# S5 products of a batch pair in rows that alternate between the two halves of TensorE, with the states one chunk late

## The chip, the cores and the metric

The kernel runs on one core of a Trainium2 chip (TensorE, VectorE, ScalarE, GpSimd and SyncE beside 16 DMA engines). The metric is the device time of one execution in microseconds.

## What is computed

A two-layer decoder trunk over 256 tokens of width 1024. Layer 0 is a SwiGLU feed-forward, a mixer made of two parallel parts (a Mamba-2 SSD and an S5), a second feed-forward and a gated input embedding; layer 1 is the same with another mixer. Only S5 is touched. In the reference it is

```python
lam_bar = jnp.exp(lam * dt)
b_bar = ((lam_bar - 1.0) / lam)[..., None] * lax.complex(b_re, b_im)
bu = jnp.einsum('blgp,gnp->blgn', ug, b_bar)
_, states = lax.associative_scan(linear_recurrence_combine, (a, bu), axis=1)
y = jnp.real(jnp.einsum('blgn,gpn->blgp', states, c)) + d_skip * ug
```

with 64 groups of 16 channels and 64 complex states per group.

## The kernel before

The 256 tokens are cut into 64 chunks of 4 steps. The 64 groups are handled as 8 batches of 8 groups; a batch is 4 (`NP`) pairs of groups, one group on partitions 0 to 63, the other on 64 to 127 (`row_half`, L496). Every S5 product on TensorE is therefore a 64x64 by 64x64 product in fp32 that uses one half of the rows and the same half of the columns of the array; in the trace one product is two weight loads and two matmuls.

There are three kinds of these products.

- **W products (L543, tile `s5w`)**: in `s5_params`, for each batch, two matrices (i = real, imaginary) are turned over by a product with the identity into the PSUM tiles `tp[0]` and `tp[1]` (tag `tr`, two buffers, which the feed-forward's transposes `ht` use too). They run during the first feed-forward, one batch per step f of it, beside that step's VectorE work on the S5 tables. There the two tiles are the two halves of the alternation.
- **v products (L684, tile `s5v`)**: in `s5_batches`, called by `recur(0)` to `recur(3)` in the mixer with two batches (e = 0, 1), 32 products per call for each of the two: chunk inputs times W, into `v[0]` and `v[1]` (tag `mm`, two buffers).
- **y products (L712 with T and U, L715 with Q and S)**: at the end of `s5_batches`, 24 products per batch and call into `y[0]` and `y[1]` (tag `mm` again). T times U is the part inside a chunk and starts each accumulation; two products (real, imaginary) of Q with the states S follow. A chunk needs the states at the end of the chunk before it, so L715 writes columns 1 to 63 of y and reads columns 0 to 62 of S.

Between v and y VectorE works, first for e = 0 and then for e = 1 (they share the single buffers `rotm` and `rw`): four operations turn v by a table (L694 to L697, `rotc`, `rots`, `rotm`), two scans carry the states along (L702, `rw`), four operations turn them back into S (`rovc`, `rovs`, `S`). ScalarE copies y into G (L719). G goes through a Gelu (L725) and DRAM, and becomes the input of the `glu` products (L758 to L760).

The engines' instruction orders are not written out by hand. A planner with a modelled clock sends out, for each engine, the instruction that is ready first in its model, earlier program text ahead of later; instructions that write the same tile keep their order. So between S5 products stand products of the projections (`pc_bc`, `pc_xs`, `pj_z`) where the planner finds them ready. `behind` (L90) adds an order without a semaphore between two instructions of one engine. On the chip each engine's queue is then fixed.

Weights come by the SP queue in 1 MB units (`wst`), are cast by ScalarE to `wh` (L61) and completed by VectorE to `wl` (L62); each unit is two of each. Beside them VectorE does the convolutions (L811) in the mixer.

Of the kernel before, what the change touches and what calls it, by code (L numbers as in the profile page):

```python
# [8 lines left out]
F32 = mybir.dt.float32  # L9
# [8 lines left out]
P = 128  # L18
# [71 lines left out]
def behind(g, ins, anchors):  # L90

    for a in anchors:
        if a.engine == ins.ins.engine:
            g.tc.add_manual_dep(ins.ins, a.name, mybir.DependencyInfo(mybir.DependencyClass.NoSync,
                                                                      mybir.DependencyReason.DATA), reason="issue_after")
# [239 lines left out]
NP = 4  # L335
# [164 lines left out]
def s5_params(g, b, half):  # L500


    nc = g.nc
    mul, add, sub = ALU.mult, ALU.add, ALU.subtract
    c3, e3, bp, z = half
    ps = slice(NP * b, NP * b + NP)
    hs = slice(NP * (b % 4), NP * (b % 4) + NP)
    tmp = [g.s5p.tile([P, 2, NP * 80], F32, tag=f"s5t{i}", name=f"s5t{i}_{b}", bufs=1) for i in range(2)]

    def cmul(out, a, br, bi, shape):  # L510

        t0, t1 = (t[:, :, 0:out.shape[2]] for t in tmp)
        for t, at, v in ((t0, 0, br), (t1, 1, bi)):
            for i in range(2):
                nc.vector.tensor_tensor(t[:, i].rearrange(shape[0], **shape[1]), a(at, i), v, op=mul)
        nc.vector.tensor_tensor(out, t0, t1, op=add)

    LE, LQ = g.s5L
    powers = lambda L, i: L[:, i, :, ps].rearrange("p t q -> p q t")
    E = g.s5p.tile([P, 2, 256], F32, tag="s5e", name=f"s5e_{b}", bufs=2)  # L520
    cmul(E, lambda at, i: bc(e3[:, (1 - at) + i, hs], 3, 4), bc(powers(LE, 0), 2, 16), bc(powers(LE, 1), 2, 16),
         ("p (q c t) -> p q c t", dict(q=NP, t=4)))
    pk = g.s5p.tile([P, PACK - PACK_PE], F32, tag="s5pk", name=f"s5pk_{b}", bufs=2)
    Q = pk[:, 768:].rearrange("p (a n) -> p a n", a=2)
    cmul(Q, lambda at, i: bc(c3[:, at + i, hs], 2, 5), bc(powers(LQ, 0), 3, 16), bc(powers(LQ, 1), 3, 16),
         ("p (q t c) -> p q t c", dict(q=NP, t=5)))
    fine, coarse = (lambda i: bc(z[:, i, hs, 0:8], 2, 8)), (lambda i: bc(z[:, i, hs, 8:16], 3, 8))
    cmul(pk[:, 0:512].rearrange("p (a n) -> p a n", a=2), lambda at, i: fine((1 - at) + i), coarse(1), coarse(2),
         ("p (q a b) -> p q a b", dict(q=NP, a=8)))
    dec = pk[:, 512:768].rearrange("p (q c) -> p q c", q=NP)  # L530
    nc.scalar.copy(dec, bc(g.s5f[2][:, ps], 2, 64))
    nc.gpsimd.memset(dec[:, :, 0:1], 0.0)
    nc.gpsimd.dma_start(g.s5dram[b][:, PACK_PE:], pk)

    def rest():
        W, K = g.s5pe
        Ev, Qv = (x.rearrange("p a (q n) -> p a q n", q=NP) for x in (E, Q))
        tp = [g.ps.tile([P, NP, 64], F32, tag="tr", name=f"s5w_{b}_{i}", bufs=2) for i in range(2)]
        for turn in range(2):
            for q in range(NP):  # L540
                for i in range(2):
                    r = row_half(turn ^ i)
                    nc.tensor.matmul(tp[i][r, q, :], Ev[r, i, q, :], g.ident[r, r], start=True, stop=True)  # L543
        for i in range(2):
            nc.scalar.copy(W[:, i], tp[i])
        kp = g.ps.tile([P, 64], F32, tag="tr", name=f"s5k_{b}", bufs=2)
        for q in range(NP):
            for i in range(2):
                nc.tensor.matmul(kp[32 * q:32 * q + 32, :], bp[:, i, hs.start + q].rearrange("p j c -> p (j c)"),
                                 Qv[:, i, q, 0:64], start=i == 0, stop=i == 1)  # L550
        nc.vector.scalar_tensor_tensor(K[:, 48:64], g.cst("fold"), g.cols("s5d")[:, b:b + 1], kp[:, 0:16], op0=mul,
                                       op1=add)
        nc.scalar.copy(K[:, 64:112], kp[:, 16:64])
        nc.gpsimd.dma_start(g.s5dram[b][:, 0:PACK_PE], W.rearrange("p a q c -> p (a q c)"))
        for st in range(4):
            nc.gpsimd.dma_start(g.s5T[b][:, st, :], K[:, 16 * (3 - st):16 * (3 - st) + 64])

    return rest
# [75 lines left out]
    return ap.rearrange("p k (s c) -> p k s c", s=4)  # L634


def s5_inputs(g, pool, U, c):

    nc = g.nc
    uT = g.lnp.tile([P, 4, NTOK], F32, tag="ln_r", name=f"uT_{c}")  # L640

    def keep(h, ps):
        k = slice(2 * h, 2 * h + 2)
        if h:
            nc.vector.tensor_copy(by_step(uT[:, k, :]), ps.rearrange("p k (c s) -> p k s c", s=4))
        else:
            nc.scalar.copy(by_step(uT[:, k, :]), ps.rearrange("p k (c s) -> p k s c", s=4))

    if c:
        project_channels(g, f"u{c}", keep)  # L650
    else:
        channel_tiles(g, pool, f"u{c}", keep)
    d = g.perm[0][c]
    nc.gpsimd.dma_start(d.rearrange("(p k) n -> p k n", k=4), uT)
    dv = d.rearrange("(q r k) (s n) -> r k q s n", q=4, k=4, s=4)
    for st in range(4):
        to = U[st:P:4, 16 * c:16 * c + 16, :].rearrange("p (k q) n -> p k q n", q=4)
        nc.gpsimd.dma_start(to, dv[:, :, :, st, :])


def s5_batches(g, pool, U, G, bs):

    nc = g.nc
    mul, add, sub = ALU.mult, ALU.add, ALU.subtract
    W, T, Q, tab, S = [], [], [], [], []
    for b in bs:
        dram = g.s5dram[b]
        W.append(pool.tile([P, 2, NP, 64], F32, tag="W", name=f"W_{b}", bufs=3))  # L670
# [5 lines left out]
        Q.append(pool.tile([P, 2, NP, 80], F32, tag="Q", name=f"Q_{b}", bufs=3))  # L676
        nc.scalar.dma_start(Q[-1], dram[:, 1280:1920].rearrange("p (a q c) -> p a q c", a=2, q=NP))
    v = [g.ps.tile([P, 2, NP, 64], F32, tag="mm", name=f"s5v_{b}", bufs=2) for b in bs]
    for turn in range(2):
        for i in range(2):  # L680
            for q in range(NP):
                for e, b in enumerate(bs):
                    r = row_half(turn ^ e)
                    nc.tensor.matmul(v[e][r, i, q, :], W[e][r, i, q, :], U[r, NP * b + q, :], start=True, stop=True)  # L684

    for e, b in enumerate(bs):
        cosT, sinT, dec = (tab[e][:, 256 * i:256 * i + 256] for i in range(3))
        w = pool.tile([P, 2, 256], F32, tag="rw", name=f"rw_{b}", bufs=1)

        def rotate(src, name, out, ops):  # L690

            c = pool.tile([P, 2, 256], F32, tag="rotc", name=f"{name}c_{b}", bufs=2)
            s = pool.tile([P, 2, 256], F32, tag="rots", name=f"{name}s_{b}", bufs=2)
            nc.vector.tensor_tensor(c, src, bc(cosT, 1, 2), op=mul)  # L694
            nc.vector.tensor_tensor(s, src, bc(sinT, 1, 2), op=mul)
            for i in range(2):
                nc.vector.tensor_tensor(out[:, i], c[:, i], s[:, 1 - i], op=ops[i])  # L697

        m = pool.tile([P, 2, 256], F32, tag="rotm", name=f"rotm_{b}", bufs=1)
        rotate(v[e].rearrange("p a q c -> p a (q c)"), "rot", m, (add, sub))  # L700
        for i in range(2):
            nc.vector.tensor_tensor_scan(w[:, i], dec, m[:, i], 0.0, op0=mul, op1=add)  # L702
        S.append(pool.tile([P, 2, NP, 64], F32, tag="S", name=f"S_{b}", bufs=2))
        rotate(w, "rov", S[-1].rearrange("p a q c -> p a (q c)"), (sub, add))
    y = [g.ps.tile([P, NP, 64], F32, tag="mm", name=f"s5y_{b}", bufs=2) for b in bs]
    for turn in range(2):
        for q in range(NP):
            for i in range(-1, 2):
                for e, b in enumerate(bs):
                    r = row_half(turn ^ e)  # L710
                    if i < 0:
                        nc.tensor.matmul(y[e][r, q, :], T[e][r, q, :], U[r, NP * b + q, :], start=True,  # L712
                                         stop=False)
                    else:
                        nc.tensor.matmul(y[e][r, q, 1:64], Q[e][r, i, q, 16:80], S[e][r, i, q, 0:63],  # L715
                                         start=False, stop=i == 1)
    for e, b in enumerate(bs):
        lo = NP * b % 16
        nc.scalar.copy(G[:, lo:lo + NP, :], y[e])  # L719
# [252 lines left out]
def ab_inputs(g, pool, s5pool, yh, yl):  # L972

    nc = g.nc
# [34 lines left out]
    U = s5pool.tile([P, 32, 64], F32, tag="U", name="U", bufs=1)  # L1009
    for c in range(2):  # L1010
        s5_inputs(g, pool, U, c)
    yT = []

    def recur(n):
        if n % 2 == 0:
            half.append(pool.tile([P, 16, 64], F32, tag="G", name=f"G_{n // 2}", bufs=1))
        s5_batches(g, s5pool, U, half[-1], (2 * n, 2 * n + 1))
        if n == 1:
            yT.append(s5_half_out(g, half[-1], 0, yh, yl))

    half = []
# [513 lines left out]
```

## Time and profile before

| | us |
|---|---|
| median of 3 runs (1238.2 to 1241.11) | 1238.76 |
| the profiled execution | 1242.7 |
| its span, first to last instruction | 1240.9 |
| W products run from | 71.3 to 202 |
| v and y products run from | 256.5 to 367 |
| busy PE / DVE / ACT / POOL | 1210.4 / 854.5 / 583.9 / 72.4 |

PE is TensorE's matmuls, DVE VectorE, ACT ScalarE, POOL GpSimd. A matmul's own duration in the trace overlaps with its neighbours', so the pace is read from the starts, or from the chain of work that ended last, which counts each stretch of time once.

### The profile page before, as it was taken

What the parts mean: (1) busy time and instruction counts of PE and PEld (TensorE: products, weight loads), DVE (VectorE), ACT (ScalarE), POOL (GpSimd) and SP (SyncE); (2) the same over time, 40 slices, a digit from 0 to 9 for tenths busy, and PEclk for the clock granted to TensorE, in tenths of its full rate; (3) what the DMA queues carried; (4) which work ended last, traced back from release to release, by engine and by line L of the source; (5) the groups of instructions that cost most, each with busy time, mean ns of one, the idle gap of its engine ahead of it and who ended that gap; (6) DMA issues with size and microseconds to landing.
All of it is one profiled execution on the core that took longest, in us unless ns stands there. A gap on an engine that the chain in (4) does not pass through costs nothing.

```text
span 1240.9 us, 17250 instructions
## 1 busy us (share of the span) xinstructions
PE 1210.4 (98%) x6786; PEld 1005.9 (81%) x6786; DVE 854.5 (69%) x1352; ACT 583.9 (47%) x866; POOL 72.4 (6%) x124
## 2 busy tenths in 40 slices
PE   7999999999998999999998999999999999999998
PEld 6877777899887878888887888888888877888886
DVE  6999894688878766555567555456779776545466
ACT  5644452545535535443435444443674625444434
POOL 0012122110203000000000000000100010000000
PEclk9999999899999999999999999999999999999999
DMA  7567676775722647555536555554633327555532
GB/s 282 203 233 251 230 243 229 267 250 175 219 95 66 220 146 252 179 198 179 195 136 203 204 190 184 198 177 168 224 135 107 133 77 247 194 186 187 192 147 102
DMA packets 44609, 232.74 MB, mean 188 GB/s; under 512 B 9680, under 2 KB 10352, under 8 KB 20848
## 3 DMA queue, kind: packets, MB, share of 16 engines
q1 hardware_dynamic: 30672, 206.06, 48.2%
q0 software_dynamic: 4688, 14.16, 3.6%
q10 hardware_dynamic: 9168, 11.42, 2.8%
q8 instruction: 53, 0.87, 0.3%
q14 instruction: 28, 0.23, 0.1%
HBM read 219.56 MB, written 12.06 MB: 187 GB/s over the span
## 4 chain that ended last, share of the span: by engine, by line
PE 90%; DVE 4%; DMA 3%; ACT 2%; issue 1%; ACTq 0%; SPq 0%; DVEq 0%
PE gu_f L178 38%; PE acc_f L72 7%; PE acc_f L71 6%; PE acc_f L70 6%; DMA wst<-in_wall_dram 2%; PE pj_z L178 2%; PE ht_f L215 2%; DVE wl L62 2%; PE s5y L715 1%; PE acc_ab L72 1%; PE acc_ab L71 1%; PE acc_ab L70 1%; PE pj_u L178 1%; PE s5w L543 1%; PE pj_hg L178 1%; PE pj_gr L178 1%
## 5 line engine op out<-in xcount | busy, mean ns | idle before, releaser
L62 DVE TENSOR_TENSOR wl<-wst,wh 128x1024 fp32r<-128x1024 f32 (+1 forms) x378 | 453.1, 1216 | 259.3 <-ACT wh L61 251.5
L61 ACT CAST wh<-wst 128x1024 fp32r<-128x1024 f32 (+1 forms) x378 | 386.9, 1047 | 359.4 <-PE gu_f L178 109.0
L71 PE MATMUL acc_f<-wl,hh_f 128*128 128x512 f32 x352 | 137.9, 392 | 0.0
L70 PE MATMUL acc_f<-wh,hh_f 128*128 128x512 f32 x352 | 137.5, 390 | 0.0
L72 PE MATMUL acc_f<-wh,hl_f 128*128 128x512 f32 x352 | 135.9, 392 | 0.0
L72 PEld LDWEIGHTS acc_f<-wh,hl_f 128*128 128x128 f32 x352 | 66.1, 188 | 13.8
L71 PEld LDWEIGHTS acc_f<-wl,hh_f 128*128 128x128 f32 x352 | 66.1, 188 | 13.6
L70 PEld LDWEIGHTS acc_f<-wh,hh_f 128*128 128x128 f32 x352 | 66.1, 188 | 13.6
L178 PE MATMUL gu_f<-wh,xh_in 128*128 128x512 f32 x176 | 71.1, 409 | 5.9 <-ACT wh L61 5.9
L178 PE MATMUL gu_f<-wh,xh_ple 128*128 128x512 f32 x176 | 70.9, 403 | 3.5 <-ACT xh_ple L112 3.5
L178 PE MATMUL gu_f<-wh,xh_ab 128*128 128x512 f32 x176 | 69.8, 397 | 0.5 <-ACT xh_ab L112 0.5
L178 PE MATMUL gu_f<-wl,xh_ab 128*128 128x512 f32 x176 | 68.8, 391 | 1.3 <-DVE wl L62 1.3
L178 PE MATMUL gu_f<-wh,xh_cd 128*128 128x512 f32 x176 | 69.9, 397 | 0.0
L178 PE MATMUL gu_f<-wl,xh_in 128*128 128x512 f32 x176 | 69.8, 400 | 0.0
L178 PE MATMUL gu_f<-wl,xh_cd 128*128 128x512 f32 x176 | 68.8, 391 | 0.7 <-DVE wl L62 0.7
L178 PE MATMUL gu_f<-wl,xh_ple 128*128 128x512 f32 x176 | 69.5, 395 | 0.0
L211 ACT ACTIVATE sg_f<-gu_f 128x256 f32<-128x256 f32 x88 | 33.8, 384 | 70.4 <-PE gu_f L178 69.1
L178 PE MATMUL gu_f<-wh,xl_ab 128*128 128x512 f32 x176 | 66.9, 391 | 0.0
L178 PE MATMUL gu_f<-wh,xl_cd 128*128 128x512 f32 x176 | 66.8, 391 | 0.0
L178 PE MATMUL gu_f<-wh,xl_ple 128*128 128x512 f32 x176 | 66.7, 391 | 0.0
L178 PE MATMUL gu_f<-wh,xl_in 128*128 128x512 f32 x176 | 66.6, 392 | 0.0
L212 DVE TENSOR_TENSOR sg_f<-sg_f,gu_f 128x256 f32<-128x256 f32 x88 | 36.7, 417 | 27.2 <-ACT sg_f L211 27.0
(466 smaller groups left out, 2387.2 us busy)
## 6 DMA issues: line engine op xcount, KB each, us to landing
wst<-in_wall_dram SPq DMA_DIRECT2D x185, 1024.0 KB, 4.8
row<-in_lnr_dram SPq DMA_DIRECT2D x12, 512.0 KB, 6.7
s5d<-s5pk POOLq DMA_DIRECT2D x8, 704.0 KB, 5.1
tab<-s5d ACTq DMA_DIRECT2D x8, 384.0 KB, 3.5
Q<-s5d ACTq DMA_DIRECT2D x8, 320.0 KB, 4.2
wst<-in_wall_dram SPq DMA_DIRECT2D x4, 512.0 KB, 6.6
s5d<-s5W POOLq DMA_DIRECT2D x8, 256.0 KB, 4.6
W<-s5d ACTq DMA_DIRECT2D x8, 256.0 KB, 3.7
```

Of the source, the lines that this page charges most:

```text
L61: ops = [nc.scalar.copy(wh[:, c], src[:, c])]
L62: ops.append(nc.vector.tensor_tensor(wl[:, c], src[:, c], f32(wh[:, c]), op=ALU.subtract))
L70: nc.tensor.matmul(out, xh, wh, start=first, stop=False)
L71: nc.tensor.matmul(out, xh, wl, start=False, stop=False)
L72: nc.tensor.matmul(out, xl, wh, start=False, stop=last)
L178: nc.tensor.matmul(ps[t], x, w, start=kh == 0 and i == 0, stop=kh == 1 and i == len(mms) - 1)
L211: nc.scalar.activation(sg, ps[t][:, 0:256], AF.Silu)
L212: nc.vector.tensor_tensor(sg, sg, ps[t][:, 256:512], op=ALU.mult)
L215: nc.tensor.transpose(tp[:, k, :], sg[:, k * P:(k + 1) * P], g.ident)
L543: nc.tensor.matmul(tp[i][r, q, :], Ev[r, i, q, :], g.ident[r, r], start=True, stop=True)
L715: nc.tensor.matmul(y[e][r, q, 1:64], Q[e][r, i, q, 16:80], S[e][r, i, q, 0:63], start=False, stop=i == 1)
```

## The change

The three kinds of S5 products get a fixed order across both tiles (`in_row`: each is put `behind` the one before it), so that neighbours alternate between the halves of the array. For v and y the pair is taken as e = 1, then e = 0. The states are held in two tiles S0, S1 for the whole mixer stage; VectorE writes states 0 to 62 into columns 1 to 63, and column 0 is zeroed once by GpSimd. The y products then all cover 64 columns, the two products with S come first and start the accumulation, and the product with U comes last. The number of products is the same.

```diff
+        g.row = ()
         for turn in range(2):
             for q in range(NP):
                 for i in range(2):
                     r = row_half(turn ^ i)
-                    nc.tensor.matmul(tp[i][r, q, :], Ev[r, i, q, :], g.ident[r, r], start=True, stop=True)
+                    in_row(g, nc.tensor.matmul(tp[i][r, q, :], Ev[r, i, q, :], g.ident[r, r], start=True, stop=True))
...
+def in_row(g, op):
+    behind(g, op, g.row)
+    g.row = (op.ins,)
...
-                for e, b in enumerate(bs):
+                for e in (1, 0):
                     r = row_half(turn ^ e)
-                    nc.tensor.matmul(v[e][r, i, q, :], W[e][r, i, q, :], U[r, NP * b + q, :], start=True, stop=True)
+                    in_row(g, nc.tensor.matmul(v[e][r, i, q, :], W[e][r, i, q, :], U[r, NP * bs[e] + q, :], start=True,
+                                               stop=True))
...
-        S.append(pool.tile([P, 2, NP, 64], F32, tag="S", name=f"S_{b}", bufs=2))
-        rotate(w, "rov", S[-1].rearrange("p a q c -> p a (q c)"), (sub, add))
+        rotate(w, "rov", S[e][:, :, :, 1:64], (sub, add), 63)
     y = [g.ps.tile([P, NP, 64], F32, tag="mm", name=f"s5y_{b}", bufs=2) for b in bs]
+    g.row = ()
     for turn in range(2):
         for q in range(NP):
-            for i in range(-1, 2):
-                for e, b in enumerate(bs):
+            for i in range(3):
+                for e in (1, 0):
                     r = row_half(turn ^ e)
-                    if i < 0:
-                        nc.tensor.matmul(y[e][r, q, :], T[e][r, q, :], U[r, NP * b + q, :], start=True,
-                                         stop=False)
-                    else:
-                        nc.tensor.matmul(y[e][r, q, 1:64], Q[e][r, i, q, 16:80], S[e][r, i, q, 0:63],
-                                         start=False, stop=i == 1)
+                    k, x = (Q[e][r, i, q, 16:80], S[e][r, i, q, :]) if i < 2 else (T[e][r, q, :], U[r, NP * bs[e] + q, :])
+                    in_row(g, nc.tensor.matmul(y[e][r, q, :], k, x, start=i == 0, stop=i == 2))
...
+    S = [s5pool.tile([P, 2, NP, 64], F32, tag=f"S{e}", name=f"S{e}", bufs=1) for e in range(2)]
+    for e in range(2):
+        nc.gpsimd.memset(S[e][:, :, :, 0:1], 0.0)
```

## Rows read from the trace of the kernel before

**Rows 1.** The page: busy time per engine, and the chain that ended last by engine.
```profile
PE 1210.4 (98%) x6786; PEld 1005.9 (81%) x6786; DVE 854.5 (69%) x1352; ACT 583.9 (47%) x866; POOL 72.4 (6%) x124
...
PE 90%; DVE 4%; DMA 3%; ACT 2%; issue 1%; ACTq 0%; SPq 0%; DVEq 0%
```

**Rows 2.** Waits of PE from 212 to 380 us: total, times, longest (first, last of six).
```profile
PE seg L833 <- ACT E L835: 1.7, 1, 1.7
...
PE xs L996 <- ACT xsT L813: 0.2, 1, 0.2
```

**Rows 3.** Stretches: length, busy PE, PEld, DVE, ACT, POOL (instructions), PE clock, DMA share, GB/s.
```profile
256.50:284.40 27.90, 27.90 (x316) 26.51 (x316) 26.11 (x51) 13.33 (x19) 2.16 (x3) 1.00 0.68 219
284.40:314.50 30.10, 30.10 (x297) 26.89 (x294) 26.07 (x59) 14.38 (x20) 0.00 (x0) 1.00 0.59 195
314.50:342.60 28.10, 27.89 (x287) 25.30 (x286) 23.13 (x43) 14.13 (x19) 6.66 (x12) 1.00 0.76 219
342.60:367.00 24.40, 24.40 (x247) 21.75 (x245) 17.82 (x33) 6.58 (x9) 0.00 (x0) 1.00 0.29 99
367.00:392.00 25.00, 19.95 (x91) 13.35 (x91) 21.96 (x52) 13.44 (x30) 8.39 (x14) 0.93 0.22 43
...
71.00:202.20 131.20, 131.20 (x872) 104.35 (x871) 115.47 (x204) 61.18 (x105) 24.36 (x50) 1.00 0.72 254
```

**Rows 4.** Tiles s5w, s5v, s5y: their matmuls, count, duration in ns, first and last start.
```profile
L543 PE MATMUL s5w<-cs,s5e x256: 218/218/267, 71.3 to 201.9; 64*64 64x64 f32 x128
...
L684 PE MATMUL s5v<-U,W x256: 218/218/267, 256.5 to 348.8; 64*64 64x64 f32 x128
...
L715 PE MATMUL s5y<-S,Q x256: 217/218/266, 271.9 to 366.8; 64*64 64x63 f32 x128
...
L712 PE MATMUL s5y<-U,T x128: 218/218/267, 262.6 to 366.5; 64*64 64x64 f32 x128
```

**Rows 5.** Chain that ended last in order of time: start, us, piece, matmuls in it.
```profile
71.33 1.08 PE s5w L543 x32
...
87.29 0.89 PE s5w L543 x16
...
256.60 2.01 PE s5v L684 x64
...
287.61 1.83 PE s5v L684 x32
...
303.53 0.37 PE s5y L715 x4
...
306.18 5.44 PE pj_z L178 x23
```

**Rows 6.** Timeline of PE around one lone y product: start, us, instruction.
```profile
262.25 0.28 PE L580 MATMUL pc_bc<-xl_f,wh 128*128 128x256 f32 x1
262.37 0.28 PE L581 MATMUL pc_bc<-xh_f,wl 128*128 128x256 f32 x1
262.57 0.32 PE L712 MATMUL s5y<-U,T 64*64 64x64 f32 x2
262.83 0.39 PE L579 MATMUL pc_bc<-xh_f,wh 128*128 128x256 f32 x1
263.05 0.28 PE L580 MATMUL pc_bc<-xl_f,wh 128*128 128x256 f32 x1
```

**Rows 7.** Timelines of DVE and PE: states S of first and last pair; a y product.
```profile
268.24 0.76 DVE L697 TENSOR_TENSOR S<-rovc,rovs 128x256 f32<-128x256 f32 x2
276.80 0.75 DVE L697 TENSOR_TENSOR S<-rovc,rovs 128x256 f32<-128x256 f32 x2
353.45 0.75 DVE L697 TENSOR_TENSOR S<-rovc,rovs 128x256 f32<-128x256 f32 x2
359.71 0.76 DVE L697 TENSOR_TENSOR S<-rovc,rovs 128x256 f32<-128x256 f32 x2
...
281.25 0.32 PE L715 MATMUL s5y<-S,Q 64*64 64x63 f32 x2
```

More of the change, by code (lines that the diff above doesn't have):

```diff
@@ L658, in s5_inputs, with s5_batches @@
         nc.gpsimd.dma_start(to, dv[:, :, :, st, :])
-def s5_batches(g, pool, U, G, bs):
+def s5_batches(g, pool, U, G, S, bs):
     nc = g.nc
     mul, add, sub = ALU.mult, ALU.add, ALU.subtract
-    W, T, Q, tab, S = [], [], [], [], []
+    W, T, Q, tab = [], [], [], []
     for b in bs:
@@ L688, in s5_batches, with rotate @@
         w = pool.tile([P, 2, 256], F32, tag="rw", name=f"rw_{b}", bufs=1)
-        def rotate(src, name, out, ops):
+        def rotate(src, name, out, ops, n=64):
             c = pool.tile([P, 2, 256], F32, tag="rotc", name=f"{name}c_{b}", bufs=2)
@@ L696, in rotate @@
             for i in range(2):
-                nc.vector.tensor_tensor(out[:, i], c[:, i], s[:, 1 - i], op=ops[i])
+                parts = (x.rearrange("p (q c) -> p q c", q=NP)[:, :, 0:n] for x in (c[:, i], s[:, 1 - i]))
+                nc.vector.tensor_tensor(out[:, i], *parts, op=ops[i])
         m = pool.tile([P, 2, 256], F32, tag="rotm", name=f"rotm_{b}", bufs=1)
-        rotate(v[e].rearrange("p a q c -> p a (q c)"), "rot", m, (add, sub))
+        rotate(v[e].rearrange("p a q c -> p a (q c)"), "rot", m.rearrange("p a (q c) -> p a q c", q=NP), (add, sub))
         for i in range(2):
             nc.vector.tensor_tensor_scan(w[:, i], dec, m[:, i], 0.0, op0=mul, op1=add)
-        S.append(pool.tile([P, 2, NP, 64], F32, tag="S", name=f"S_{b}", bufs=2))
-        rotate(w, "rov", S[-1].rearrange("p a q c -> p a (q c)"), (sub, add))
+        rotate(w, "rov", S[e][:, :, :, 1:64], (sub, add), 63)
     y = [g.ps.tile([P, NP, 64], F32, tag="mm", name=f"s5y_{b}", bufs=2) for b in bs]
+    g.row = ()
     for turn in range(2):
         for q in range(NP):
-            for i in range(-1, 2):
-                for e, b in enumerate(bs):
+            for i in range(3):
+                for e in (1, 0):
                     r = row_half(turn ^ e)
-                    if i < 0:
-                        nc.tensor.matmul(y[e][r, q, :], T[e][r, q, :], U[r, NP * b + q, :], start=True,
-                                         stop=False)
-                    else:
-                        nc.tensor.matmul(y[e][r, q, 1:64], Q[e][r, i, q, 16:80], S[e][r, i, q, 0:63],
-                                         start=False, stop=i == 1)
+                    k, x = (Q[e][r, i, q, 16:80], S[e][r, i, q, :]) if i < 2 else (T[e][r, q, :], U[r, NP * bs[e] + q, :])
+                    in_row(g, nc.tensor.matmul(y[e][r, q, :], k, x, start=i == 0, stop=i == 2))
     for e, b in enumerate(bs):
@@ L1016, in recur @@
             half.append(pool.tile([P, 16, 64], F32, tag="G", name=f"G_{n // 2}", bufs=1))
-        s5_batches(g, s5pool, U, half[-1], (2 * n, 2 * n + 1))
+        s5_batches(g, s5pool, U, half[-1], S, (2 * n, 2 * n + 1))
         if n == 1:
```

## Prediction

> **What bounds the kernel now.** I read first the busy times and the chain that ended last: TensorE is busy 98% of the span and carries 90% of the chain [rows 1]. That is an average, so next come the two stretches that the change touches. From 71 to 202 us (W products) and from 256.5 to 367 us (v and y products) PE is busy 131.20 of 131.20 and 110.3 of 110.5 us at the full clock [rows 3]. The list of what PE waited for confirms it: from 212 to 380 us it holds six entries, 1.7 to 0.2 us each, and none of them is an S5 product [rows 2]. So in both stretches time taken off PE is time off the end, as long as no other engine comes up behind it. The candidate is DVE: 115.47 of 131.2 us in the first stretch, and in the four S5 turns of the second 26.11 of 27.9, 26.07 of 30.1, 23.13 of 28.1 and 17.82 of 24.4 us [rows 3]. Its idle time there, 1.8 + 4.0 + 5.0 + 6.6 = 17.4 us, is what can be gained before it becomes the bound.
>
> **What a product costs in and out of a row.** The trace of before happens to contain both orders. In the first pair all v products were free at once and stand alternating: 64 matmuls in 2.01 us, 31.4 ns each. A later pair's v came one tile after the other, so that one half of the array got them all: 32 matmuls in 1.83 us, 57.2 ns each. W products show the same: 32 alternating in 1.08 us (33.8 ns), 16 on one half in 0.89 us (55.6 ns). A run of y products of one batch, from 303.53 to the next projection at 306.18, holds 46 matmuls (48 less the two issued earlier): 57.6 ns each [rows 5]. So two halves that take turns overlap, and one half alone does not.
>
> A second cost is the change between S5 and other products. Around a lone product the projections start at 262.37, 262.83 and 263.05 where their pace is 0.12 us (262.25 to 262.37): 0.68 instead of 0.24, 0.44 us more; the two matmuls account for 2 x 57 ns = 0.11, so a change there and back costs about 0.33 us [rows 6]. The Trainium skill (TensorEngine Tiling (Array Packing), Key Properties) says that a change of the tiling mode drains the array while tiles of one mode run side by side, which these rows agree with; it gives no price.
>
> **Part by part.**
> - *v row.* Of 256 matmuls [rows 4] 64 alternate already [rows 5]; 192 x (57.2 - 31.4) ns = 5.0 us off PE.
> - *y row.* 384 matmuls [rows 4], all on one half at a time: 384 x (57.6 - 31.4) ns = 10.1 us. No row shows accumulating products alternating; between 31.4 and 57.6 ns I take the low end, because accumulation costs nothing extra on one half (57.6 against 57.2).
> - *W row.* The first batch's 32 and about half of the last batch's alternate; 208 x (55.6 - 33.8) ns = 4.5 us. The row starts with i = 0, whose PSUM tile comes free first, so its first product may still stand alone; I count no saved changes here (up to 8 x 0.33 = 2.6 us more).
> - *Changes.* Between the first v and the last y start (256.5 and 366.8 us) [rows 4] PE's timeline has 24 separate stretches of v and y. With one row per v and per y of four pairs, 8 remain: 16 x 0.33 = 5.3 us [rows 6]. Nothing in `in_row` forbids other products in between; that the rows stay whole follows from all their inputs being there once e = 1 can begin, which the first v row shows.
> - *64 instead of 63 columns, U product last.* Both forms have a median of 218 ns [rows 4]; nothing. The lone T products that ran ahead now wait for S too, which is within the counts above.
> - *States one column later.* DVE's last operations write 252 of 256 columns, strided; 8 pairs at 0.76 us [rows 7], changed by some per cent at most: under 0.3 us either way, nothing taken.
> - *Two memsets on POOL.* POOL is busy 2.16 us in the first S5 turn and idle in the next [rows 3], and the zeros are needed only with the first y at about 270 us. Hidden; without that cover about 1 us.
> - *The added wait.* y of e = 0 now also waits for S of e = 1, which DVE finishes 8.6 us later in the first pair and 6.3 us later in the last [rows 7]. Behind it on PE stand whatever products the planner put there, and the copy to G, hence the PSUM buffers of the next v. In the trace a y product comes 3.7 us after its states are done (281.25 against 277.55) [rows 7]: the planner thinks DVE slower than it is, so the row should seldom stall PE's queue, and projections fill the time in between.
>
> PE's own sum: 5.0 + 10.1 + 5.3 = 20.4 us in the mixer and 4.5 us in the feed-forward, 24.9 in all.
>
> **What is late next.** In the feed-forward DVE has 15.7 us idle of 131, more than 4.5; I keep the 4.5. In the mixer PE would save per turn about 3.8 (y and 4 changes, v being in order), then 5.5 three times, against DVE's idle 1.8, 4.0, 5.0, 6.6 us [rows 3]. DVE cannot use its idle time in full: the S5 chain hands over from PE to DVE and back twice per turn. I take about seven tenths of 17.4, 12 us. The reason to stop there is that DVE reached 26.11 of 27.9 us in the best turn, 94%; at 94% in all turns its 93.1 us of work would take 99, a gain of 11.5. After 367 us the SSD part runs with DVE at 21.96 of 25 us and PE no longer full [rows 3]; it is only moved forward. Sum: 4.5 + 12 = 16.5 us.
>
> On the profiled execution (1240.9 span and 1.8 around it) that is 1242.7 - 16.5 = 1226.2. That execution lies 3.9 us above the median of the runs shown, so the forecast for the median is 1238.76 - 16.5 = 1222.3.
>
> The Trainium skill's same page (Performance Considerations, PSUM Bottleneck) warns that tiling speeds up TensorE but not the emptying of PSUM, which may become the bottleneck. Here that is DVE's reading of v and ScalarE's copy of y, and the 94% row speaks for it. By that rule alone the gain would be the 16.5 us; without it the 24.9.
>
> **Rivals.**
> 1. *PE's whole sum arrives.* DVE's operations that nobody waits for (weight completions ahead of need) slide into the idle time after 360 us, and DVE does not limit. For: PE waits on no DVE in this stretch [rows 2]. Against: 20.4 us is more than DVE's 17.4 us idle [rows 3]. 1238.8 - 24.9 = 1214.
> 2. *The S5 chain eats the mixer's part.* Two v and y rows per turn, each after both batches, put PE and DVE in series; DVE's other work fills only part. The gain is the feed-forward's 4.5 us: 1234. For: e = 0 no longer starts early. Against: PE found other work in all gaps of these turns so far, busy 24.40 of 24.40 us even in the last [rows 3].
> 3. *Slower: PE stands still between the states of e = 0 and e = 1.* If the planner puts no projections there, each of four y rows waits for the difference, 8.6 to 6.3 us, mean 7.5: 30 us lost against 24.9 gained, 1244. It decides from a mean wait of 24.9 / 4 = 6.2 us per y row. Against: the 3.7 us lead of DVE and the filler.
> 4. *The rows do not form, or accumulating products do not overlap.* Then only v, W and some changes count, 5.0 + 4.5 + 2 = 11.5 us: 1227. If none of it forms: 1239.
>
> **How the numbers follow.** Forecast as summed, 1216 to 1230 (with the partly formed rows of rival 4, which end there): 0.62. Rival 1: 0.20. Rival 2: 0.10. Rival 3: 0.05. No rows at all: 0.03. A measurement of this kernel tells about 0.3%, 3.7 us, from no change, so faster means under 1235.0. Faster: 0.62 + 0.20 + 0.06 of rival 2 = 0.88; same 0.07; slower 0.05. The range from 1210 to 1234 takes in the whole sum with four saved changes of the W rows and reaches to rival 2; about 0.15 is left out.
>
> **What would show it.** v rows of 64 matmuls in about 2.0 us, y rows of 96 in about 3.0, W rows of 32 in about 1.1, each in one piece. DVE above 90% in the S5 turns with less idle time before `wl`. The last y product at about 350 us from the start instead of 367, 4 to 5 of it already gone at 216 us. Wrong if y rows run at 57 ns, if PE shows waits for S in the list, or if the feed-forward's DVE delays weights.

## The result, and the profile after

| | before | after |
|---|---|---|
| median, us | 1238.7 | 1247.97 (1247.02 to 1251.51) |
| ratio to before, 95% interval | | 1.0076 (1.0053 to 1.010) |
| profiled execution / its span | 1242.7 / 1240.9 | 1247.0 / 1245.2 |

The change makes the kernel 0.5 to 1.0% slower where 16.5 us of gain were forecast. PE did get less work. The page of the changed kernel, the busy times and the chain by engine (as [rows 1]):

```profile
PE 1192.0 (96%) x6786; PEld 989.8 (79%) x6786; DVE 855.0 (69%) x1352; ACT 584.3 (47%) x866; POOL 73.2 (6%) x126
...
PE 75%; DVE 10%; issue 3%; DMA 2%; ACT 2%; ACTq 0%; DVEq 0%
```

PE is busy 18.4 us less than before, yet only 75% of the chain runs through it instead of 90%; DVE (10% instead of 4%) and plain waiting (`issue`, 3% instead of 1%) have taken most of the rest. The rows formed, though the W rows and the second v row with a first product that stands alone. The chain in order of time shows a y row of 96 matmuls in 2.94 us (30.6 ns each, 31.4 forecast), and the last one in 5.47:

```profile
351.72 2.94 PE s5y L722 x96
...
369.62 5.47 PE s5y L722 x96
```

Where the time went is in the list of PE's waits from 218 to 420 us, which had no S5 entry and nothing above 1.7 us before (its first entry is that of [rows 2]):

```profile
PE s5y L722 <- issue: 9.6, 1, 9.6
PE glu L764 <- ACT yh L745: 5.1, 1, 5.1
PE glu L765 <- DVE yl L746: 3.9, 1, 3.9
```

Here `issue` means that the profile names no releaser. The stretches (columns as in [rows 3]: length, busy PE, PEld, DVE, ACT, POOL, clock, DMA share, GB/s):

```profile
292.30:327.40 35.10, 35.10 (x341) 31.42 (x340) 33.27 (x70) 19.19 (x27) 0.00 (x0) 1.00 0.58 196
327.40:357.30 29.90, 19.16 (x236) 16.91 (x235) 17.56 (x31) 10.39 (x15) 6.67 (x12) 0.83 0.62 183
...
357.30:369.60 12.30, 2.75 (x69) 2.48 (x69) 10.03 (x20) 0.00 (x0) 0.00 (x0) 0.80 0.01 2
369.60:375.00 5.40, 5.38 (x96) 5.29 (x96) 0.25 (x1) 0.00 (x0) 0.00 (x0) 0.51 0.01 3
```

In the second turn (first line) PE is full and DVE nearly so, 33.27 of 35.1 us. In the third PE stands still for 10.7 us in four pieces, then for 9.6 more: 20.3 us, somewhat more than the 18.4 it had saved. By then the projections are used up: the last ends at 337.7 us, before the change at 354. Of the 10.7 us, 8.9 are waits of `glu` products, which the queue has ahead of the third y row, for their casts `yh` and `yl`; the states that this row needs are done at 348.4 us, the row starts at 351.7. The 9.6 us lie between the last v row and the last y row, which starts at 369.62, 0.5 us after the start of DVE's last states operations. What is left there is one chain: v row, DVE, y row. After 9.58 us of standing the last y row meets a granted clock of 0.51 (the 1.2 GHz level) and takes 5.47 us instead of 2.94.

The chain can be followed on DVE, by its first reading of v in a pair and its last states operation. The hand-over between turns 1 and 2 ended before the change (its start is 276.80, [rows 7]) with

```profile
286.26 0.69 DVE L694 TENSOR_TENSOR rotc<-s5v,tab 128x512 f32<-128x512 f32 x1 [1.51 <-PE s5v L684]
```

and after it this hand-over, the first reading of v and the end of the last pair's states are (timeline of DVE)

```profile
261.30 0.68 DVE L703 TENSOR_TENSOR rotc<-s5v,tab 128x512 f32<-128x512 f32 x1
...
279.62 0.74 DVE L707 TENSOR_TENSOR S<-rovc,rovs 128x252 f32<-128x252 f32 x2
...
297.05 0.68 DVE L703 TENSOR_TENSOR rotc<-s5v,tab 128x512 f32<-128x512 f32 x1
...
369.10 0.75 DVE L707 TENSOR_TENSOR S<-rovc,rovs 128x252 f32<-128x252 f32 x2
```

From the last states of a pair to the first reading of the next pair's v pass 17.4 us (279.62 to 297.05), then 16.1 and 11.8, 45.3 in all; before it was 9.5, 10.5 and 8.6 (28.5). The turns on DVE between them became shorter (72.2 to 62.5 us), so from the first reading to the last states it is 107.8 us instead of 100.7 (258.97 to 359.71).

The other loss lies ahead of that. The layer norm's transposes after the first feed-forward (timeline of PE) began before the change at the first, and now begin at the second of these:

```profile
217.61 1.29 PE L142 MATMUL tp_ln<-cs,x_ln 128*128 128x128 f32 x8 [1.69 <-DVE x_ln L138]
```
```profile
220.24 1.42 PE L142 MATMUL tp_ln<-cs,x_ln 128*128 128x128 f32 x8 [1.71 <-DVE x_ln L138]
```

Together: feed-forward +2.6, from there to the first v reading -0.3, the S5 chain +7.1, all that follows -5.1: +4.3 us, which is 1245.2 - 1240.9. The -5.1 is not explained. Of it 2.2 us come up to the layer norm behind the mixer, and 2.9 in the part of the kernel from there to 1018 us, which is the same in all kernels here and lasts 555.4 to 560.5 us in the traces of this case, longest in that of before. So the two profiles differ by 4.3 us where the medians differ by 9.3: the profiled execution of before is 3.9 us above its median, that of the change 1.0 below.

### The profile page after: what moved, and what is told of

It is laid out like the page before. It is cut to its first block, busy times and chain, and to the rows that moved or that the text cites. A ratio compares the mean times of both kernels' runs of the same rounds, so it can differ in the third digit from the quotient of the medians.

```text
span 1245.2 us, 17248 instructions
## 1 busy us (share of the span) xinstructions
PE 1192.0 (96%) x6786; PEld 989.8 (79%) x6786; DVE 855.0 (69%) x1352; ACT 584.3 (47%) x866; POOL 73.2 (6%) x126
## 4 chain that ended last, share of the span: by engine, by line
PE 75%; DVE 10%; issue 3%; DMA 2%; ACT 2%; ACTq 0%; DVEq 0%
PE gu_f L178 33%; PE acc_f L72 6%; PE acc_f L70 6%; PE acc_f L71 6%; DVE wl L62 2%; DMA wst<-in_wall_dram 2%; PE ht_f L215 1%; PE acc_ab L70 1%; PE acc_ab L71 1%; PE acc_ab L72 1%; PE pj_u L178 1%; PE pj_hg L178 1%; PE pj_gr L178 1%; PE pj_hi L178 1%; PE pj_gv L178 1%
## 5 line engine op out<-in xcount | busy, mean ns | idle before, releaser
L72 PEld LDWEIGHTS acc_f<-wh,hl_f 128*128 128x128 f32 x352 | 66.1, 188 | 13.7
```

The source lines that it names most:

```text
L72: nc.tensor.matmul(out, xl, wh, start=False, stop=last)
```

## The experiments

Theory A after the result: alternation gains what was forecast, and the joint wait (one row for two tiles or batches) loses it. A row cannot go beyond its first product before both of its tiles (or batches) are ready, and all that would have followed from the first one waits with it. Its rivals stand in the expectations (B: the loss is only passed on; C: two halves cannot write one PSUM bank; D: DVE bounds the mixer in any order; E: it is the v row; F, G, H as named there). Each ratio is to runs of the kernel before in the same group; their medians there are 1238.4 to 1239.6 us. The last column comes from one profiled execution of each kernel.

| kernel | edit | median, us | ratio to before | S5 on DVE, first v read to last states, us |
|---|---|---|---|---|
| before | | 1238.7 | | 100.7 |
| the change | | 1248.0 | 1.0076 (1.0053 to 1.0100) | 107.8 |
| w_row | W row alone | 1243.4 | 1.0036 (1.0014 to 1.0058) | 100.5 |
| v_row | v row alone | 1247.0 | 1.0068 (1.0051 to 1.0084) | 108.4 |
| y_row | y row alone | 1239.0 | 1.0004 (0.9985 to 1.0023) | 101.4 |
| y_wait | y waits for both, no alternation | 1240.0 | 1.0019 (1.0006 to 1.0032) | 99.2 |
| vy_rows | v and y rows | 1242.4 | 1.0019 (0.9999 to 1.0039) | 104.2 |
| w_half | W alternates inside a tile | 1236.3 | 0.9975 (0.9957 to 0.9994) | 100.5 |
| all_half | W, v, y alternate inside a tile | 1223.1 | 0.9868 (0.9832 to 0.9904) | 92.5 |
| half_late | all_half with late states | 1225.9 | 0.9894 (0.9865 to 0.9922) | 94.2 |
| vhalf_yrow | half_late with the y row | 1237.8 | 0.9990 (0.9970 to 1.0010) | 101.5 |
| w_one | W row, both tiles in one buffer | 1229.1 | 0.9931 (0.9908 to 0.9953) | 99.8 |
| after_one | the change with w_one | 1234.3 | 0.9975 (0.9957 to 0.9994) | 104.0 |
| after_dt | the change, dt_ps elsewhere | 1247.9 | 1.0080 (1.0054 to 1.0107) | 104.8 |
| before_noscan | no scans | 1231.4 | 0.9958 (0.9943 to 0.9974) | 94.3 |
| after_noscan | the change, no scans | 1233.6 | 0.9970 (0.9948 to 0.9992) | 93.0 |
| one_half | w_one and all_half's v and y | 1219.3 | 0.9845 (0.9811 to 0.9879) | 92.5 |

**w_row.** The kernel before with `in_row` in the W products only.

> The kernel before with the W row alone. Theory A (a row holds the PSUM buffers of both its tiles until its last product, so the feed-forward's transposes and the next products come later): the layer norm after the first feed-forward begins 2 to 3 us later than before (before: first transposes 217.6 us, changed kernel 220.2), PE shows waits on the K copy, median 1240 to 1243. Theory B (the loss is all in the mixer, the feed-forward's shift comes from there or from chance): the transposes come 3 to 5 us earlier, median 1234 to 1236.

0.36% slower, 1243.4 us, just above A's range; the transposes of the layer norm start at 220.35 us, as in the changed kernel, PE waits 1.5 us for the copy of K, and the S5 chain that follows is as long as before. A holds, B falls: the W row alone makes the feed-forward longer. What happens there, in the changed kernel's PE timeline (second batch):

```profile
87.66 0.33 PE L544 MATMUL s5w<-cs,s5e 64*64 64x64 f32 x2
...
96.12 1.14 PE L544 MATMUL s5w<-cs,s5e 64*64 64x64 f32 x30
...
102.18 0.45 PE L550 MATMUL s5k<-s5pk,s5bp 128*32 128x64 f32 x16
```

The first product (two matmuls) writes one `tr` tile at 87.66, and the row goes on only at 96.12, with the other tile. For those 8.5 us one of the two `tr` buffers is held by a single product; before, all 8 products of the first tile (16 matmuls) went at once. (A batch has 16 W products, 32 matmuls, and likewise 16 v products, not the 32 named ahead.) The next user of the buffers, `s5k`, now comes 5 us behind the row as a stretch of its own instead of right behind it, and the feed-forward's transposes come behind that.

**w_one.** The same row, but with both tiles in one buffer, one PSUM bank:

```diff
-        tp = [g.ps.tile([P, NP, 64], F32, tag="tr", name=f"s5w_{b}_{i}", bufs=2) for i in range(2)]
+        both = g.ps.tile([P, 2, NP, 64], F32, tag="tr", name=f"s5w_{b}", bufs=2)
+        tp = [both[:, i] for i in range(2)]
```

> The W row alone, in the changed kernel's order, but both of its tiles lie in one PSUM bank, so that it takes one tr buffer instead of two. Theory A (the W row loses because it holds both tr buffers until its last product): the loss of w_row (1243) turns into a gain, layer norm transposes before 217 us, median 1234 to 1238. Rival C (halves cannot share a bank) or H (the row itself delays the feed-forward): 1240 to 1245.

More than expected: 1229.1 us, 14 us faster than w_row. Each row is whole, and `s5k` stands right behind it (PE's timeline, w_one; then the layer norm's transposes):

```profile
90.68 1.15 PE L545 MATMUL s5w<-cs,s5e 64*64 64x64 f32 x32
91.76 0.45 PE L551 MATMUL s5k<-s5pk,s5bp 128*32 128x64 f32 x16
...
210.42 1.29 PE L142 MATMUL tp_ln<-cs,x_ln 128*128 128x128 f32 x8 [0.58 <-DVE x_ln L138]
```

The feed-forward ends 7.2 us earlier than before. The same order of the same 16 products loses with two buffers and gains with one: it was the second buffer. H and C fall. The other kernels repeat it: the transposes start at 217.6 to 218.0 us in the six that have the W products of before, at 219.3 to 221.8 in the four with the row in two buffers, at 209.7 to 210.4 in the three with the row in one. Why it is 7.2 us and not the 4.5 of the prediction was not tested; `s5k` right behind each row leaves fewer changes between S5 and other products, for which the prediction had named up to 2.6 us.

**w_half.** W products with the halves as the innermost loop, each tile by itself (`for i`, `for q`, `for turn`, no `in_row`).

> The kernel before with the W products in an order that alternates the halves of the array inside one tile (i outer, q, then the two halves), no order across the two tiles. Theory A: alternation without a joint wait keeps the buffers moving, 32 products of a batch take 0.9 to 1.1 us instead of 1.8, feed-forward 3 to 5 us shorter, median 1234 to 1236. Rival C (two halves of the array cannot write one PSUM bank at the same time, as a note of the Trainium skill, TensorEngine Tiling (Array Packing), section Restrictions and Gotchas, says): 16 matmuls still take 0.9 us, median 1238 to 1240.

3.3 us faster in the medians, A's range missed by 0.3 us. 16 matmuls of a tile now take 0.68 us where they took 0.96 (at 87.3 us, PE's timeline), with both halves of the array writing one bank in pairs that start 7 ns apart; the transposes start at 214.7 us, 2.9 earlier. In the three other kernels with this W order they start at 215.7, 216.2 and 217.1, so the gain is 0.5 to 2.9 us. The note of the Trainium skill that was the ground of rival C (TensorEngine Tiling (Array Packing), Restrictions and Gotchas: row tiles cannot access the same bank at the same time) does not hold for these products, which write different partitions of the bank.

**vy_rows.** The changed kernel with the W products as before.

> The changed kernel without the W row (v rows, y rows, late states). Theory A (the rows put the two batches' VectorE work and the PSUM buffers in series, PE runs out of projections before the fourth turn): the last y product is 5 to 6 us later than before (before 367), PE has waits of 15 to 20 us between 320 and 400 us, median 1241 to 1245. Theory B (the mixer's loss is only what the feed-forward handed on): last y before 365, median 1225 to 1236.

1242.4; A's range, and its sign: PE waits 17.7 us before y rows here. The interval just touches no change, and the last y product at 368.2 us is later by less than the 5 to 6 us that A wanted. B falls all the same (it wanted 365 or less).

**v_row, y_row, y_wait.** One row at a time, and the joint wait without alternation (`for e in (1, 0)` outside, `turn` next, chained by `in_row`).

> The kernel before with the v row alone. Theory A (a joint wait costs what it holds back): both v tiles are free soon after the last y, so the row waits little; 192 matmuls leave at half the pace, 5 us off PE, last y product 2 to 6 us earlier than before's 367, median 1234 to 1238. Theory E (the v row is where the loss arises): median 1240 to 1245.

> The kernel before with the y row alone (with the late states and the T product last). Theory A: y of e = 0 is held until the states of e = 1 (6 to 9 us later on VectorE), the next v with it; last y product not earlier than 364 although PE does 10 us less, PE waits of 8 to 18 us before y products or in the projections behind, median 1238 to 1245. Theory E (the v row makes the loss): median 1228 to 1234.

> The y products wait for both batches' states as in the changed kernel, but do not alternate: all 24 of e = 1, then all 24 of e = 0, each half by half; v and W as before. The joint wait alone. Theory A: nothing is gained on PE and the wait is paid, 8 to 20 us slower than before: 1246 to 1260, and about 10 us slower than y_row. Theory D (VectorE's work bounds the turns, the wait is hidden): within 4 us of before, 1236 to 1243.

Two of the three went against A as it stood: v_row lies above even E's range, y_wait in D's. The v row, which I thought harmless, loses most: 8.2 us, although it was to take 5 us off PE. Before, v of e = 0 slips in beside the y products of the turn before; in the row it waits until the last y buffer is copied out, and the hand-overs grow from 28.5 to 42.6 us. PE's timelines show it, before and in v_row:

```profile
311.54 0.62 PE L684 MATMUL s5v<-U,W 64*64 64x64 f32 x7
```
```profile
310.00 0.33 PE L691 MATMUL s5v<-U,W 64*64 64x64 f32 x2
...
320.64 0.91 PE L691 MATMUL s5v<-U,W 64*64 64x64 f32 x22
```

It is what the W row did: one product holds one of the two `mm` buffers, here from 310.0 us, and the rest follow at 320.6, 2.7 us after the copy of the last y has freed the other (317.6 to 318.0). The changed kernel's second v row has the same pattern (289.3 and 292.3 us).

The y row comes out even, in A's range. And the wait alone (y_wait) costs 1 us, 2.4 by the ratio, not 8 to 20; y_row, where PE was to do 10 us less, cannot be told from it (the intervals overlap). The third kernel with this wait and the v products outside a row, vhalf_yrow below, also ends there: 1239.0, 1240.0 and 1237.8 us. So with this joint wait the stage hardly goes by PE's work any more: what PE saves there hardly shows.

**before_noscan, after_noscan.** The 16 scans are left out, and S is made from `rotm` instead of `rw`; the states are then not carried along.

```diff
-        for i in range(2):
-            nc.vector.tensor_tensor_scan(w[:, i], dec, m[:, i], 0.0, op0=mul, op1=add)
...
-        rotate(w, "rov", S[e][:, :, :, 1:64], (sub, add), 63)
+        rotate(m, "rov", S[e][:, :, :, 1:64], (sub, add), 63)
```

> The kernel before without the 16 scans on VectorE (0.6 us each, 10 us in all): the S5 states are left out, the rest of S5 runs on the unscanned values. Theory A (PE bounds the mixer before, the S5 chain is hidden): gain under 4 us, 1235 to 1239. Theory D (VectorE bounds it): gain of 7 to 10, 1229 to 1232.

> The changed kernel without the same 16 scans. Theory A (the serial chain v, VectorE, y bounds the mixer after the change): gain of 7 to 14 us against the changed kernel, 1234 to 1241. Theory D' (something else in PE's order bounds it): gain under 4 us, 1244 to 1248.

10 us off DVE give 14.4 us in the changed kernel and 7.0 us before (5.2 by the ratio). A's first half missed, and the median lies in D's range: the stage was not bound by PE alone before the change, and DVE's chain was worth half of what was taken from it. Its second half holds: after the change the chain is the bound (1.06% between the two ratios, 13 us). That this is more than the 10 us taken off goes with less standing, 4.9 us before the last y row instead of 9.6, and a granted clock of 0.99 instead of 0.94 from 240 to 400 us.

**after_dt.** `dt_ps`, the one tile that comes between the first and the second turn in the `mm` buffers, takes `tag="tr"`.

> The changed kernel with the PSUM tile of the time steps (dt_ps, used once between the first and the second turn) taken from the two tr buffers instead of the two mm buffers that v and y share. Theory A (the second v row stands behind dt_ps and VectorE's reading of it, because it needs both mm buffers): the second v row starts 3 to 6 us earlier after the first y row (changed kernel: 285.9 to 292.3), median 1241 to 1245. Theory G (the hand-over is VectorE's order, not the buffer): the same 1247 to 1249.

No change, 1247.9, in G's range. The buffer as the single reason for the long first hand-over falls: it went from 17.4 to 11.3 us, but the turns on DVE grew and the end stayed.

**all_half.** All three kinds alternate inside a tile, each batch for itself; for v:

```diff
-    for turn in range(2):
-        for i in range(2):
-            for q in range(NP):
-                for e, b in enumerate(bs):
-                    r = row_half(turn ^ e)
+    for e, b in enumerate(bs):
+        for i in range(2):
+            for q in range(NP):
+                for turn in range(2):
+                    r = row_half(turn)
```

> The kernel before with W, v and y products all alternating inside one tile; no rows across batches, states not late, T first as before. Theory A (the alternation gains, the joint wait loses): v and y of e = 0 keep their early start, PE work falls by about 18 us as in the changed kernel and the S5 turns stay overlapped: last y product at 352 to 360, median 1222 to 1232. Theory D (VectorE's S5 work bounds the mixer, whatever the order): last y at 362 to 370, median 1233 to 1240. Rival C (one bank): as before, 1238 to 1240.

1223.1, 1.3% faster than before, in A's range. That it is nearly the time forecast for the change is in part chance: the feed-forward gives 1.9 us here, not 4.5. Alternation gains here, where no batch waits for the other. One batch's v takes 0.93 to 1.08 us instead of 1.83 (chain), and PE is as full as it was (a stretch of all_half; from 300 to 350 us it is 49.63 of 50):

```profile
277.30 0.93 PE s5v L684 x32
```
```profile
256.50:300.00 43.50, 43.50 (x470) 40.14 (x469) 43.08 (x93) 23.77 (x34) 0.00 (x0) 1.00 0.65 219
```

DVE works 43.08 of 43.5 us here, 99%, so the 94% at which the forecast stopped was not its limit. The hand-overs are 6.8, 7.6 and 5.4 us, 19.7 in all, and the last y product starts at 349.5 us. D falls as a reason for the loss.

**half_late, vhalf_yrow.** all_half with the changed kernel's states and order of T; then with its y row in place of half_late's y products.

> all_half with the states one chunk late, 64 columns and the T product last, each batch still on its own. Theory A: the late states cost nothing, the joint wait did; 1221 to 1226, as all_half (1223). Theory F (the T product that ran ahead and the 63 columns mattered): 1228 to 1240.

> half_late with the changed kernel's y row in place of its y products: W and v alternate inside a tile, y waits for both batches. Theory A (each joint wait lengthens the hand-over from the states to the next turn by some 3 us): 8 to 14 us slower than half_late, 1233 to 1240. Theory E (only the v row loses): as half_late, 1222 to 1229.

1225.9 and 1237.8, both in A's ranges. The first cannot be told from all_half: the late states, the 64 columns and T at the end cost little or nothing. It has all of the change but the rows across tiles and batches, and it is 22 us faster than the change (1.8% between the ratios): the loss comes with the rows. The second has the same products, which alternate too, but in one row for both batches, so that y of e = 0 is held until the states of e = 1. This joint wait costs 12 us; the chain on DVE is 7.3 us longer and PE waits 9.3 us before a y row.

**after_one.** The changed kernel with w_one's single bank.

> The changed kernel with its two W tiles in one PSUM bank, all else as changed. Theory A (the loss in the feed-forward is the second tr buffer): layer norm transposes near 211 instead of 220 us, and the whole 8 to 10 us arrives at the end: 1236 to 1241. Theory H (the mixer takes the gain back): 1243 to 1248.

1234.3, 13.7 us faster than the change (12.5 by the ratios) by one tile's place, and faster than before. The transposes start at 210.3 us, and the S5 chain stays long at 104.0 us: the loss of the feed-forward undoes by itself.

**one_half.** w_one with all_half's v and y.

> w_one and all_half together: the W row in one PSUM bank, v and y alternating inside each batch's tile. Theory A (the two gains lie in different stages and add: feed-forward 7 us earlier, mixer some 15 us shorter): 1212 to 1220. Rival (the mixer is bounded by VectorE by then, and takes no more): 1221 to 1228.

1219.3, the fastest, 1.55% (1.2 to 1.9) below before, in A's range, though its interval overlaps that of all_half. Layer norm transposes at 209.73 us, the last y product at 344.0 instead of 366.8, PE busy 99.63 of 100 us there (stretch of one_half):

```profile
245.00:345.00 100.00, 99.63 (x1160) 89.94 (x1160) 93.76 (x185) 49.75 (x70) 9.63 (x16) 1.00 0.65 212
```

## Why the prediction was wrong

- *PE's paces were right.* v 2.0 us, y 2.94 us, W 1.1 to 1.4 us for a row, nine stretches of v and y instead of 24 where eight were forecast; 18.4 us of busy time gone where 20.4 + 4.5 were summed (the last y row alone, at the lower clock, takes 2.5 us more than the others). The memsets took 0.1 us each, at 219 us, hidden as forecast. all_half shows that such a saving can arrive: 15.6 us in the medians.
- *The v row failed.* It was costed as PE's time alone, 5.0 us of gain, with no wait. By itself it loses 8.2 us and makes the chain on DVE 7.7 us longer (108.4 instead of 100.7), because v of e = 0 no longer starts beside the last y products.
- *"The added wait" failed.* I asked whether PE's queue would stall behind a y row and priced that at nothing, because DVE had a lead of 3.7 us and projections filled PE. Both were so for two turns (the first y row starts 2.5 us after its states). But the wait does not cost where PE fills it; it costs because the next v, and with it DVE's next turn, starts later. The hand-overs were the quantity to add up: 28.5 us before, 45.3 after. The waits of v and y rows, priced at 0, are +7.1 us on the chain with PE's saving already in it; the y row's alone are 12 us in vhalf_yrow.
- *"What is late next" failed.* I took DVE's idle time as a stock to be used and 94% as its limit. all_half reaches 99% in a stretch, and the changed kernel has DVE idle for 10.4 us in one piece. What bounds this stage after the change is the length of the series v, DVE, y, copy, not DVE's amount of work.
- *The W row failed.* It was costed as PE's time alone, 4.5 us of gain, with the remark that its first product may stand alone. It did, in seven of eight batches, and the missing question was who wants the buffer that it holds meanwhile: +2.6 us in the feed-forward instead of -4.5.
- *Rivals.* Rival 2 named the mechanism (v and y rows put PE and DVE in series) but let the mixer end even, at 1234, and gave it 0.10. Rival 3, the slower end, had the wrong place: PE stands still not between the states of e = 0 and e = 1 of each turn, but at the end, once the projections are used up (10.7 and 9.6 us, of which 4.0 lie between the last pair's two states). Rival 1 fell, rival 4 fell.
- *What stays open.* The parts do not add up: v_row alone loses 8.2 us, with y_row 2.8 (ratio 1.0019); and the y wait costs 12 us in vhalf_yrow but hardly shows in y_wait. The planner makes every queue anew for every kernel, and the delays between a release and its place in PE's queue (2.5 us for the first y row after, 3.7 before) move with it. Which of the delays inside a hand-over is the planner's was not settled; after_dt excluded only one buffer, and in the third hand-over `glu` products stand ahead of the y row and of the v row. That the feed-forward's loss in w_row also holds more changes between modes (`s5k` on its own, some 0.33 us each) is argued, not measured.

## What to carry to other kernels

Before two pieces of work are joined to make one of them cheaper, list what starts early today from the first piece alone (a buffer freed, a next turn begun), and add up that hand-over from the trace; a full engine is only full as long as filler work lasts. The same saving without a joint wait is worth looking for first: here two halves that alternate inside one tile need neither the second tile nor the second batch.

## What the runs showed of the hardware

Two 64x64 products on opposite halves of the array run side by side even when both write one PSUM tile (different partitions of it): 32 matmuls of one tile in 0.93 us, 29 ns each, against 57 ns on one half (all_half). They start in pairs, 7 ns apart, with 58 ns from pair to pair (277.540, 277.546 and 277.598 us). Accumulating products do too: pairs 6 to 7 ns apart, 58 ns from pair to pair, within one tile (all_half, 296.3 us), and 96 matmuls across two tiles in 2.94 us. And a y row that came after 9.58 us of standing took 5.47 us at a granted clock of 0.51.
